# First keys and queries of a hard-max attention kernel: loaded in fp32 from the sync queue and rounded on VectorE and ScalarE instead of cast by the GpSimd queue

## The chip, the cores and the metric

The kernel runs on one core of one Trainium2 chip. The metric is the device time of one execution in microseconds (us), and lower is better. Times below are medians of several executions with their lowest and highest value; no execution showed the slower state of the chip, and for one core a single run's state can't be told ("unknown"). A profiled execution gives a span that is 1.7 to 2.2 us shorter than the time of the same execution, so spans are compared with spans and times with times. What is read from one trace (starts of tiles, landings) belongs to that one execution.

Engine names as the profile has them: PE is TensorE (matmuls), PEld its weight loads, DVE is VectorE, ACT is ScalarE, POOL is GpSimd, SP is SyncE. A name with a q (SPq, POOLq) is an engine's sequencer: it issues transfers, waits on semaphores and so on.

## The reference

```python
def reference(q, k, v):            # B=4, Sq=Sk=4096, D=128, all fp32
    logits = np.matmul(q, k.transpose(0, 2, 1))
    best = np.argmax(logits, axis=-1)
    b_idx = np.arange(q.shape[0])[:, None]
    return v[b_idx, best, :].astype(np.float32)
```

For each query the one key with the largest dot product is found, and its row of v is the output.

## The kernel before

Queries are handled in 128 tiles of 128 rows, 32 for each batch. A tile is screened in fp16: PE multiplies it with the keys, ScalarE evicts (A and E below), VectorE folds the result (W) and takes the eight largest entries (MAX8, written to TOP). GpSimd then gathers the candidates' rows for a more exact comparison, and at the end the rows of v that won. Keys of batch 0 are transposed on PE against an identity matrix. Query tiles 0 to 3 too; all later query tiles are transposed by DMA (`turn_q`), from the sync queue.

The parts that matter here, cut:

```python
    def load_k(b, h, x, y):                       # fp32 in DRAM, fp16 in SBUF: cast by GpSimd's queue
        kb = k[b].rearrange("(h p n) d -> p h n d", p=P, n=16)
        nc.gpsimd.dma_start(out=natk[b % 2][:, h, x:y], in_=kb[:, h, x:y])

    def put_k(b, h):                              # differences of keys, stored for the later gathers
        ...
        nc.vector.tensor_tensor(out=kd[:, h], in0=src[:, :, 1:4, :], in1=..., op=OP.subtract)
        nc.sync.dma_start(out=kb16[:, h], in_=kd[:, h].rearrange("p g f d -> p (g f d)"))

    load_k(0, 0, 0, 16)                           # first half of batch 0's keys
    load_q(0, 0, 4)                               # query tiles 0 to 3
    ...                                           # warm-up matmuls on zeros
    masks.make_identity(nc, ident)
    load_k(0, 1, 0, 8)                            # second half, two pieces
    load_k(0, 1, 8, 16)
    load_q(0, 4, 8)
    load_q(0, 8, NQT)
    ...
    for z in (FR, FQ, FK, FV):
        nc.gpsimd.memset(z, 0)
    ...
    def turn_q(b, x, y):                          # query tiles x..y-1, transposed by DMA
        nc.sync.dma_start_transpose(out=qT[b % 2][:, x * P:y * P]..., in_=natq[b % 2][:, x:y, :]...)

    def dpart(t, x):                              # pd matmuls of tile t, ScalarE's eviction to A
        ...
        mm(ps, t, 1 + 2 * x, True)
        nc.scalar.activation(out=A, in_=ps, func=AF.Abs)
    ...
    trn_half(1, 0, ALL, by_act)                   # first half of the keys: PE transposes, evictions
    trn_half(3, 0, ALL, by_dve)
    trn_half(0, 0, ALL, by_act)
    trn_q(0, 4, by_dve)
    trn_half(2, 0, ALL, by_act)
    put_k(0, 0)
    for u in (1, 3, 0, 2):
        trn_half(u, 1, (0, 1))                    # second half, first piece
    trn_half(1, 1, (2, 3), by_act)                # second half, second piece
    ...
    dpart(0, 0)
    dpart(0, 1)
    ...                                           # main loop; in its first 8 steps GpSimd issues
            load_part(1, it, 4)                   #   batch 1's keys, again casting
        if it == 1:
            turn_q(0, 4, 8)
```

## Time and profile before

| | before |
|---|---|
| time, median of 3 runs | 443.31 us (443.29 to 443.79) |
| profiled span | 441.9 us |
| first screening matmul (pd of tile 0) | 12.34 us |
| first MAX8 | 20.72 us |
| first DMA transpose of queries: issued, landed | 11.86, 18.78 us |
| last scatter starts on GpSimd | 437.69 us |
| software DMAs (GpSimd's DMA instructions in the trace) | 309 |

First the DMA view of the kernel before for 14 to 18 us: packets, MB and share of the 16 engines for GpSimd's queue (q0) and the sync queue (q1).

```profile
q0 software_dynamic: 353, 0.39, 71.9%
q1 hardware_dynamic: 680, 0.50, 44.0%
```

Both queues move data in these 4 us.

### The profile page before, as it was taken

Reading aid. Unit: us, or ns where it says so; the run is one execution under the profiler, and the core shown is the slowest. Engines: PE = TensorE matmul, PEld = TensorE weight load, DVE = VectorE, ACT = ScalarE, POOL = GpSimd, SP = SyncE. Lnnn points to the kernel's source line nnn. Section 1 sums busy time; section 2 is a strip of 40 time slices with the busy share of each in tenths; the row PEclk is TensorE's granted clock in tenths of the full one; section 3 lists DMA queues with packets and bytes.
Section 4 is the critical chain, followed back from the end, with each engine's and each line's share of the span. In section 5 each row is a group of like instructions: output and inputs, shape, how many; then the busy total and the mean of one; then the engine's idle time right before and its main releaser. Section 6 shows DMA issues by size and latency. Waiting matters only on the chain.

```text
span 441.9 us, 6163 instructions
## 1 busy us (share of the span) xinstructions
PE 378.9 (86%) x1830; PEld 168.0 (38%) x1830; DVE 405.9 (92%) x734; ACT 375.6 (85%) x437; POOL 306.2 (69%) x335
## 2 busy tenths in 40 slices
PE   7999999999999999999998889999889997892100
PEld 4444444444444444444443334443333333330100
DVE  2688999999999999999999999999999999999840
ACT  2899999999999999999998889999989998892000
POOL 8413456677768786777777776777777777777673
PEclk9999999999999999999999999999999999998555
DMA  7933999463326999743336993453322332323432
GB/s 123 202 101 65 157 148 139 106 130 80 108 58 134 180 163 170 147 114 91 84 94 142 173 162 100 96 132 107 85 82 84 90 89 80 88 80 102 122 113 53
DMA packets 52868, 50.54 MB, mean 114 GB/s; under 512 B 34136, under 2 KB 40890, under 8 KB 52832
## 3 DMA queue, kind: packets, MB, share of 16 engines
q0 software_dynamic: 19072, 33.87, 39.2%
q1 hardware_dynamic: 33760, 16.26, 14.5%
q8 instruction: 14, 0.23, 0.2%
q14 instruction: 22, 0.18, 0.2%
HBM read 40.05 MB, written 14.55 MB: 124 GB/s over the span
## 4 chain that ended last, share of the span: by engine, by line
ACT 37%; issue 20%; DVE 13%; PE 12%; POOL 8%; DMA 8%; POOLq 0%; ACTq 0%; DVEq 0%; SPq 0%
ACT A L234 31%; ACT E L247 6%; DVE TOP L264 4%; PE psn L225 4%; POOL vr L342 4%; PE pd L225 4%; POOL kg L282 4%; DVE W L260 4%; PE psn L244 3%; DMA vr<-in_v_dram,win 3%; DMA natk<-in_k_dram 2%; DMA out_dram<-vr 1%; DMA kg<-k,cand 1%; DVE prod L300 1%; DMA vr<-in_v_dram,win_w 1%
## 5 line engine op out<-in xcount | busy, mean ns | idle before, releaser
L234 ACT ACTIVATE A<-pd 128x1024 f16<-128x1024 f32 x256 | 260.8, 1046 | 12.5 <-PE pd L225 12.0
L282 POOL DMA_INDIRECT kg<-k,cand x126 | 126.4, 1003 | 80.0 <-DVE cand L276 48.7
L260 DVE SCALAR_TENSOR_TENSOR W<-psn,E 128x1024 int16<-128x1024 f32 x128 | 167.1, 1306 | 7.4 <-ACT E L247 5.3
L225 PE MATMUL psn<-kT,qT 128*128 128x512 f16 x512 | 151.9, 378 | 11.4 <-ACT A L234 4.0
L225 PE MATMUL pd<-kT,qT 128*128 128x512 f16 x512 | 151.9, 379 | 8.7 <-ACT A L234 8.2
L264 DVE MAX8 TOP<-W 128x8 f32<-128x1024 f32 x128 | 157.0, 1227 | 0.0
L225 PEld LDWEIGHTS <-qT 128*128 128x128 f16 x1024 | 97.9, 97 | 151.8 <-issue 62.0
L342 POOL DMA_INDIRECT vr<-in_v_dram,win x126 | 125.9, 999 | 40.0 <-issue 36.1
L244 PE MATMUL psn<-A,identh 128*128 128x512 f16 x512 | 152.1, 378 | 0.0
L247 ACT ACTIVATE E<-psn 128x1024 int16<-128x1024 f32 x128 | 132.6, 1036 | 2.3 <-PE psn L244 1.5
L244 PEld LDWEIGHTS <-identh 128*128 128x128 f16 x512 | 49.6, 97 | 60.7
L300 DVE TENSOR_TENSOR prod<-kg,natq 128x768 f16<-128x768 f16 x63 | 34.8, 554 | 0.4 <-DMA kg<-k,cand 0.4
L205 ACT ACTIVATE kT<-uk 128x256 f16<-128x256 f32 x48 | 20.6, 429 | 1.5 <-PE uk L202 1.5
L305 DVE TENSOR_TENSOR p<-prod 128x768 f16<-128x768 f16 (+1 forms) x36 | 18.1, 502 | 0.1
L310 DVE TENSOR_REDUCE D<-p 128x12 f32<-128x384 f16 (+1 forms) x36 | 17.7, 492 | 0.1
L201 PE MATMUL uk<-identh,natk 128*128 128x128 f16 x96 | 15.8, 218 | 0.0
L484 PE MATMUL fp_e<-n_e,tri 128*128 128x1 f32 x2 | 0.6, 364 | 13.5 <-DVE n_e L482 13.5
L202 PEld LDWEIGHTS <-natk 128*128 128x128 f16 x96 | 9.3, 97 | 7.2 <-issue 5.1
L308 DVE TENSOR_TENSOR p<-p 128x384 f16<-128x384 f16 (+1 forms) x36 | 11.9, 330 | 0.1
L66 POOL DMA_DIRECT2D natk<-in_k_dram x19 | 11.3, 599 | 0.8 <-POOLq L890 0.8
L201 PEld LDWEIGHTS <-natk 128*128 128x128 f16 x96 | 9.3, 98 | 5.6
L69 POOL DMA_DIRECT2D natq<-in_q_dram x15 | 9.2, 614 | 0.0
(152 smaller groups left out, 140.1 us busy)
## 6 DMA issues: line engine op xcount, KB each, us to landing
out_dram<-vr SPq DMA_DIRECT2D x31, 256.0 KB, 2.1
natq<-in_q_dram POOLq DMA_DIRECT2D x12, 256.0 KB, 5.3
natk<-in_k_dram POOLq DMA_DIRECT2D x10, 256.0 KB, 4.5
k<-kd SPq DMA_DIRECT2D x18, 128.0 KB, 3.7
k<-natk POOLq DMA_DIRECT2D x6, 384.0 KB, 6.4
kg<-k,cand POOLq DMA_INDIRECT x126, 3.0
vr<-in_v_dram,win POOLq DMA_INDIRECT x126, 2.7
natk<-in_k_dram POOLq DMA_DIRECT2D x8, 128.0 KB, 5.7
```

Source lines behind the costliest of these rows:

```text
L201: nc.tensor.matmul(out=o, lhsT=natk[b % 2][:, h, 4 * m + x, :], rhs=identh, start=True, stop=False)
L205: nc.scalar.activation(out=kT[b % 2][:, c:c + 256], in_=ps, func=AF.Copy)
L225: nc.tensor.matmul(out=ps[:, n * 512:(n + 1) * 512], lhsT=qT[b % 2][:, qt * P:(qt + 1) * P], rhs=kT[b % 2][:, u * 1024 + n * 512:u * 1024 ...
L234: nc.scalar.activation(out=A, in_=ps, func=AF.Abs)
L244: nc.tensor.matmul(out=ps[:, n * 512:(n + 1) * 512], lhsT=identh, rhs=A[:, n * 512:(n + 1) * 512], start=False, stop=True)
L247: nc.scalar.activation(out=E, in_=ps, func=AF.Relu, scale=QSCALE)
L260: nc.vector.scalar_tensor_tensor(out=W_t[t % NW].bitcast(I16)[:, 1::2], in0=ps, scalar=QSCALE, in1=E, op0=OP.mult, op1=OP.max)
L264: nc.vector.max(out=TOP[:, t, :], in_=W_t[t % NW].bitcast(FP32))
L282: near_q.append(lambda j=j: nc.gpsimd.indirect_dma_start(out=kg[:, j].rearrange("p f d -> p (f d)"), out_offset=None, in_=k16[t0 // NQT], ...
L300: nc.vector.tensor_tensor(out=prod[:, i:i + h], in0=kg[:, i:i + h], in1=natq[b % 2][:, x + i - b * NQT:x + i + h - b * NQT, :].unsqueeze(2 ...
L305: nc.vector.tensor_tensor(out=p1, in0=prod[:, :, :, 0:64], in1=prod[:, :, :, 64:128], op=OP.add)
L342: late_q.append(lambda j=j: nc.gpsimd.indirect_dma_start(out=vr[:, j, :], out_offset=None, in_=v_flat, in_offset=IOA(ap=win[:, i + j:i + j ...
```

## The change

The first keys and queries shall not wait for the casting loads. They are loaded unconverted by the sync queue and rounded to fp16 on chip. GpSimd's zero fills go to ScalarE, which is idle then. The other query loads are issued behind the constants, and the subtraction with its store (`put_k(0, 0)`) moves behind the first screening matmuls.

```diff
-    load_k(0, 0, 0, 16)
-    load_q(0, 0, 4)
+    wide_k = bp.tile([P, 2, 16, P], FP32, tag="wide_k")
+    wide_q = bp.tile([P, 4, P], FP32, tag="wide_q")
+    first_k = k[0].rearrange("(h p n) d -> p h n d", p=P, n=16)
+    nc.sync.dma_start(out=wide_k[:, 0, 0:8], in_=first_k[:, 0, 0:8])
+    nc.sync.dma_start(out=wide_k[:, 0, 8:16], in_=first_k[:, 0, 8:16])
+    nc.sync.dma_start(out=wide_q, in_=q[0].rearrange("(p t) d -> p t d", p=P)[:, 0:4])
+    nc.sync.dma_start(out=wide_k[:, 1, 0:8], in_=first_k[:, 1, 0:8])
+    nc.sync.dma_start(out=wide_k[:, 1, 8:16], in_=first_k[:, 1, 8:16])
...
     masks.make_identity(nc, ident)
-    load_k(0, 1, 0, 8)
-    load_k(0, 1, 8, 16)
-    load_q(0, 4, 8)
-    load_q(0, 8, NQT)
...
-    for z in (FR, FQ, FK, FV):
-        nc.gpsimd.memset(z, 0)
+    nc.gpsimd.memset(FR, 0)
+    for z in (FK[:, 0], FK[:, 1], FK[:, 2], FQ, FV):
+        nc.scalar.activation(out=z, in_=wz[:, 0:z.shape[1]], func=AF.Copy)
+    load_q(0, 4, 8)
+    load_q(0, 8, NQT)
...
+    def narrow(put, h, x, y):
+        put(natk[0][:, h, x:y], wide_k[:, h, x:y])
+
+    narrow(by_dve, 0, 0, 8)
+    narrow(by_dve, 0, 8, 16)
+    by_act(natq[0][:, 0:4], wide_q)
     trn_half(1, 0, ALL, by_act)
     trn_half(3, 0, ALL, by_dve)
     trn_half(0, 0, ALL, by_act)
+    narrow(by_dve, 1, 0, 8)
     trn_q(0, 4, by_dve)
     trn_half(2, 0, ALL, by_act)
-    put_k(0, 0)
+    narrow(by_dve, 1, 8, 13)
+    narrow(by_act, 1, 13, 16)
...
     dpart(0, 0)
     dpart(0, 1)
+    put_k(0, 0)
```

## The prediction

> **What bounds the kernel now.** I read the page first (busy shares), then the windows view cut at the stages, then the chain that ended last, then the timeline of the first 16 us, where the change acts, and the DMA view of the same stretch.
>
> The columns of the windows view are: stretch, length, then busy us (and count) of PE, PEld, DVE, ACT and POOL, then clock, DMA share and GB/s.
>
> ```profile
> 12.34:27.40 15.06, 14.87 (x67) 6.35 (x67) 11.03 (x13) 14.44 (x16) 3.96 (x8) 1.00 1.02 196
> 27.40:60.00 32.60, 31.10 (x163) 14.34 (x161) 29.34 (x35) 32.60 (x42) 15.49 (x18) 1.00 0.59 101
> 60.00:110.00 50.00, 48.89 (x244) 22.13 (x243) 49.83 (x70) 50.00 (x62) 33.25 (x35) 1.00 0.66 117
> 170.00:250.00 80.00, 76.78 (x378) 34.47 (x377) 79.93 (x126) 77.46 (x94) 59.66 (x62) 1.00 0.57 122
> ```
>
> From 12.34 us the kernel runs at throughput: PE is busy 14.87 of 15.06 us, then ACT 32.60 of 32.60, then VectorE 79.93 of 80.00 deep in the run. The change touches none of the work in those stages; it touches what lies before 12.34. So the question is when the first screening matmul (pd, L225) starts. The chain of waits answers (start, us, what):
>
> ```profile
> 3.67 7.54 DMA natk<-in_k_dram
> 11.21 0.05 issue
> 11.26 0.23 PE tk L183
> ...
> 12.34 0.61 PE pd L225 x2
> 12.94 0.02 issue
> 12.96 1.03 ACT A L234
> ```
>
> The last half-load of batch 0's keys lands at 11.21 us; 1.08 us later, after 16 transposing matmuls and one eviction, pd starts. The timeline shows what else stands in the way:
>
> ```profile
> 1.19 5.24 PE L113 MATMUL warm<-wz 128*128 128x512 f16 x14 [1.19 <-DVE wz L109]
> 6.65 0.23 PE L183 MATMUL tk<-identh,natk 128*128 128x128 f16 x1 [0.22 <-DMA natk<-in_k_dram]
> 9.04 0.95 DVE L75 TENSOR_TENSOR kd<-natk 128x1536 f16<-128x1536 f16 x1
> 9.94 0.23 PE L183 MATMUL tk<-identh,natk 128*128 128x128 f16 x1 [0.83 <-DMA natk<-in_k_dram]
> 11.26 0.23 PE L183 MATMUL tk<-identh,natk 128*128 128x128 f16 x1 [0.25 <-DMA natk<-in_k_dram]
> 11.86 1.36 SPq L208 DMA_TRANSPOSE qT<-natq  x1
> 11.91 1.89 DVE L193 CAST kT<-tk 128x512 f16<-128x512 f32 x3 [1.93 <-PE tk L184]
> ```
>
> The warm-up matmuls hold PE until 1.19 + 5.24 = 6.43, so the first half of the keys could be used at most 0.22 us earlier than it is. The second half costs two waits, for loads at 9.94 and 11.26. So the start is DMA-bound, on the second half only.
>
> **What the Trainium skill says.** (1) DMA: Bandwidth & Descriptors, section "SWDGE vs HWDGE vs iDMA": a cast inside a transfer is for the GpSimd queue only, plain copies go to the sync queue. The trace agrees in form: all natk and natq loads are on POOLq and write fp16. That is why the change needs a rounding step. (2) Same page, "iDMA fabric": a plain load stream from SP with 4 KiB rows alone reached 408.7 GB/s. No plain load stream is in this trace, but the casting loads moved 201 to 205 GB/s of fp16 between 4 and 6 us (windows of one us), which is 402 to 410 GB/s of fp32 read. (3) Same page, "Queues, rings and completion order": each DMA engine takes turns between the queue rows it has work for, so sync loads share engines with whatever GpSimd issues. (4) VectorE: DVE Perf Modes, "Mode 2×_2P": a one-source op from SBUF to SBUF yields two elements per cycle even for fp32 (clock 0.96 GHz). The trace agrees: the 128x128 fp32-to-fp16 copy of the identity starts 0.14 us before the next instruction. At two per cycle its data take 128/1.92 = 0.067 us, leaving 0.07 us of overhead, the same as MAX8 leaves (1.14 us in the chain against 1024/0.96 = 1.07).
>
> **The change, part by part.**
>
> *Loads.* Removed from GpSimd: four casting issues before the iotas (natk 0.73, natq 0.59, natk 1.10 for two; some 2.4 us), with two more natq issues (1.08 us) moved behind the constants. Added: five plain loads on sync. They can be issued right after the start barrier, at about 0.75 us (ACT starts at 0.73, VectorE at 0.86), at some 0.35 to 0.42 us of queue time each (the q32 load later in the run takes 0.425). That one's neighbour, a 256 KB output store, takes a median 2.1 us to landing; at 400 GB/s its bytes are 0.65 us, so about 1.4 us is fixed. The loads are 524, 524, 262, 524 and 524 KB in fp32, 2.36 MB. At 400 GB/s, from 0.75 + 1.4 = 2.15, they land at 3.5, 4.8, 5.4, 6.7 and 8.0 us. The last lands 3.2 us before today's 11.21.
>
> *Rounding.* Keys on VectorE: 128x1024 costs 1024/1.92 + 0.07 = 0.61 us, 128x640 costs 0.40. On ACT: q 128x512 is like today's 128x512 eviction, 0.60; the last 128x384 is about 0.48. The first two key copies (done by 5.5) and the q copy (done by 6.0) lie in front of 6.43, where PE is still warming: free. The other three are on the path.
>
> *Simulated start.* PE begins transposing at 6.43 instead of 6.65, so today's events of the first half all move by -0.22. VectorE: eviction of u=3 ends about 8.2, key copy 8.2 to 8.8, q eviction (0.65) to 9.45, 640-wide copy to 9.87. ACT: third eviction ends 9.74 - 0.22 = 9.52, then the 384-wide copy to 10.0. PE does the first eight tiles from 8.85 to 10.0, partly waiting for PSUM buffers. So the last sixteen matmuls can start at about 10.05 instead of 11.26: **1.2 us earlier**. With the same 1.08 us behind them pd starts at 11.13. The gate is now VectorE and ACT, not the transfer, which has about 1.5 us of slack there.
>
> *Zero fills.* GpSimd loses 0.19 + 1.37 + 0.19 = 1.75 us of memsets; ACT gets three of 512 and two of 128 columns, some 3 x 0.5 + 2 x 0.2 = 1.9 us between the table load's end (2.01) and 4.0, before q arrives: free. GpSimd was not on the path either, except through its issues.
>
> *put_k moved.* The 0.95 us subtraction leaves 9.04, makes room for the key copies, and runs after the three last evictions, from about 12.5 to 13.5. VectorE waits for the first E until 16.77 today (2.75 us idle): free on VectorE. But the order of instructions shows its store ahead of the query transposes on the sync queue.
>
> **Sum:** 443.3 - 1.2 + 0 to 0.3 for what follows (below) = **442.1 us**.
>
> **Rivals.**
>
> *A. The query transposes become the wait.* They were issued at 11.86; now they sit behind the store that waits for put_k, so 13.5 + 0.35 = 13.85. Today's first one lands late:
>
> ```profile
> qT<-natq SPq DMA_TRANSPOSE x1, 6.9
> ```
>
> 13.85 + 6.9 = 20.75. Query tile 4 is first used three rounds after pd; today that is 21.75 (rounds of 2.75 us), or 9.4 after pd, hence 20.5 in the new kernel. A stall of 0.2 us, if landing stays slow. Against it: GpSimd's batch-1 and query loads now start at about 7.5 instead of 13.0 for the former, so the burst that slows the transposes should end near 17.6 (3.8 MB at 400 GB/s after 8.0) instead of 20.8; over the run the median is 5.3 us. I give it 0 to 0.3 us; at worst 1 us, leaving 443.1.
>
> *B. Plain fp32 loads are slower.* The same page of bytes is read, but twice as much is written. If the rate were 270 GB/s, the last load would land at 2.15 + 8.7 = 10.9, the gate would be 11.3 to 11.5, and the gain gone: 443.3 to 443.6. For it: between 6 and 9 us today's loads fall to 103 to 157 GB/s of fp16 with the engines fully busy, for a reason I do not see. Against: the 4 to 6 us figure, and the skill's. One in eight.
>
> *C. VectorE copies run at one element per cycle.* Then 1024 columns cost 1.14 us and 640 cost 0.74; the gate moves to 10.8, the gain shrinks to 0.4: 442.9. The identity copy speaks against it.
>
> *D. The shift does not reach the end.* GpSimd gathers or a late wait could absorb it. But every later start follows from a cross-engine wait or a queue position, none from absolute time, and VectorE is full from 60 to 400 us, so a start d earlier should end d earlier. I allow 0.3 us either way for different interleaving.
>
> **Range and chances.** 1.2 us is 0.27% of the time. Main case 441.8 to 442.4; with A or C up to 443; better if the gate falls to the loads' own time (down to 441.3). Range 441.3 to 443.1. Two per cent would be 8.9 us, more than anything before 12.34 could give short of removing most of it, and no rival costs a third of that: within 2% at 0.98.
>
> **What would show it right or wrong.** In the new profile: the sync loads land by about 8 us (B wrong); key copies of 128x1024 show about 0.6 to 0.7 us (C wrong); the last transposing group starts near 10.05 and waits for ACT or VectorE rather than a DMA; the first pd is at 11.1; no PE wait on qT near 20.5 (A wrong; if seen, its length is A's cost); and every stage after that has the same lengths. It is wrong if pd starts at 11.1 and the end has not moved, or if pd is not earlier than 12.

## More of the kernel before

"Software DMAs" are the transfers that GpSimd issues; in the kernel before, all loads that convert fp32 to fp16 under way are of this kind.

GpSimd issued the casting loads of batch 1's keys only from 13.02 on (timeline):

```profile
13.02 3.28 POOL L66 DMA_DIRECT2D natk<-in_k_dram  x6
```

Then the end: the timeline's last work of GpSimd, and the source view of the kernel's closing line (operation, count, duration in ns as minimum/median/maximum, first and last start).

```profile
437.69 1.02 POOL L541 DMA_INDIRECT out_dram<-FV,rowk_e  x1 [3.77 <-DMA out_dram<-vr]
L901 POOLq DRAIN  x3: 46/109/3253, 437.5 to 441.6; - x3
```

The longest of GpSimd's three DRAIN instructions takes 3.253 us. Its record starts at 437.46, just ahead of the last scatter's, and it is what the closing barrier waits for, apart from 0.37 us behind its end, in which SyncE is later: GpSimd goes on at 441.08.

## The result

| | before | after | difference |
|---|---|---|---|
| time, median of 4 runs of the same rounds | 443.3 (442.78 to 443.79) | 449.94 (449.31 to 450.36) | +6.6 us |
| profiled span | 441.9 | 448.5 | +6.6 |
| first pd matmul | 12.34 | 11.57 | −0.77 |
| MAX8 of tile 0 | 20.72 | 19.96 | −0.76 |
| MAX8 of tile 4 | 32.33 | 36.07 | +3.74 |
| MAX8 of tile 64 | 209.43 | 213.13 | +3.70 |
| MAX8 of tile 124 | 398.36 | 401.83 | +3.47 |
| last scatter starts | 437.69 | 440.49 | +2.80 |
| longest DRAIN of GpSimd | 3.253 | 7.342 | +4.09 |
| software DMAs | 309 | 305 | −4 |

The ratio of the times is 1.0149, with a 95% interval of 1.0131 to 1.0167: within the 2% that count as the same, but outside the predicted range by a wide margin, and slower instead of faster. Ratios here and below are the mean time of one kernel's fast runs over that of the other's of the same rounds, so they are not quite the ratio of the medians quoted.

The start did become earlier, as intended. The windows view of the changed kernel, cut at the same times as the prediction's (same columns), shows in which stage that was lost:

```profile
12.34:27.40 15.06, 11.27 (x45) 4.39 (x43) 8.75 (x11) 11.08 (x12) 0.37 (x1) 0.90 1.11 200
60.00:110.00 50.00, 48.92 (x245) 22.15 (x243) 49.83 (x71) 50.00 (x62) 33.42 (x36) 1.00 0.67 122
170.00:250.00 80.00, 76.74 (x375) 34.49 (x375) 79.97 (x123) 78.16 (x95) 59.98 (x62) 1.00 0.56 121
```

PE was busy 14.87 us of the first stretch before; now it is 11.27, with 45 matmuls instead of 67, at a mean clock of 0.90. In the later stages PE and VectorE are busy as long as before, within 0.05 us. The chain of waits names the loss:

```profile
2.14 6.52 DMA wide_k<-in_k_dram
8.68 0.74 DVE natk L198
...
11.15 1.89 DVE kT L198 x3
13.04 0.86 DVE kd L75
...
14.14 0.12 SPq L78
14.30 10.40 DMA qT<-natq
24.70 0.05 issue
24.75 1.03 PE pd L230 x2
```

The first query transpose is issued at 14.30, takes 10.40 us and lands at 24.70, and tile 4's pd matmul starts on it. The timeline shows the queue order: the store of the key differences, then the transposes.

```profile
13.93 0.33 SPq L78 DMA_DIRECT2D k<-kd  x1
14.30 5.79 SPq L213 DMA_TRANSPOSE qT<-natq  x2
```

The wait itself stands in the waits view (us in total, times, longest):

```profile
PE pd L230 <- DMA qT<-natq: 3.6, 1, 3.6
```

Tile 3's rounds would have let tile 4's pd start near 11.57 + 9.41 = 20.98 (9.41 is the distance in the kernel before, 21.75 − 12.34), so 24.75 is 3.77 us late. With the 0.76 us gained that makes +3.01 for tile 4, and its MAX8 shows +3.74. The remaining 0.73 us fits what follows the stall: for about 3 us (24.4 to 27.6) matmuls take 0.63 us in place of 0.38, at a granted clock of 0.50. From there the delay stays nearly constant for 360 us.

Why the transposes took 10.4 us is visible in the DMA view of the changed kernel, 14 to 18 us:

```profile
q0 software_dynamic: 375, 0.53, 91.6%
...
k<-kd SPq DMA_DIRECT2D x1, 384.0 KB, 7.5
qT<-natq SPq DMA_TRANSPOSE x1, 10.4
```

There is no line of q1 at all: in these 4 us not one packet of the sync queue moved, though a store and a transpose were queued on it from 13.93 and 14.30. GpSimd's queue had the engines for 91.6% of the time. It had been given its next loads early (timeline), because GpSimd was relieved of issues and zero fills:

```profile
9.52 3.19 POOL L66 DMA_DIRECT2D natk<-in_k_dram  x6
```

These are batch 1's keys, not needed for a long time, 3.5 us earlier than before. They took a median 11.9 us to land, against 5.8 before (of those whose landing is on record). The store's first packet starts at 18.3 us, and the transposes' small packets pass only from 20 us on.

At the other end of the program, the timeline's last scatter and the closing line of the changed kernel read:

```profile
440.49 1.02 POOL L546 DMA_INDIRECT out_dram<-FV,rowk_e  x1 [3.38 <-DMA out_dram<-vr]
L916 POOLq DRAIN  x3: 51/109/7342, 440.3 to 448.2; - x3
```

Again three DRAINs, but the longest takes 7.342 us. The two losses add up: the last scatter is 2.80 us later, the drain 4.09 us longer, and of the 0.37 us that GpSimd used to go on waiting for SyncE 0.05 are left: 2.80 + 4.09 − 0.32 = 6.57, the lateness of the barrier (447.65 against 441.08) and of the span. The scatter itself is not slower: by its semaphore it has landed at 442.69, and the drain goes on for 4.9 us more, in which the trace shows no packet of GpSimd's queue (the last one starts at 442.35); before, the scatter landed at 439.96 and the drain ended 0.75 us later. The tail also won something back, +3.47 at tile 124 against +2.80 at the last scatter; why was not looked into.

### The profile page after: what moved, and what is told of

Same layout as the page of the kernel before. It is cut to its first block, busy times and chain, and to the rows that moved or that the text cites. A ratio compares the mean times of both kernels' runs of the same rounds, so it can differ in the third digit from the quotient of the medians.

```text
span 448.5 us, 6172 instructions
## 1 busy us (share of the span) xinstructions
PE 378.8 (84%) x1830; PEld 168.2 (38%) x1830; DVE 409.2 (91%) x738; ACT 378.1 (84%) x444; POOL 302.3 (67%) x328
## 3 DMA queue, kind: packets, MB, share of 16 engines
q0 software_dynamic: 18496, 32.69, 36.5%
q1 hardware_dynamic: 34480, 18.62, 15.9%
## 4 chain that ended last, share of the span: by engine, by line
ACT 40%; issue 19%; DVE 15%; PE 15%; DMA 7%; POOL 1%; POOLq 0%; ACTq 0%; SPq 0%; DVEq 0%
ACT A L239 33%; ACT E L252 7%; PE pd L230 5%; DVE TOP L269 5%; PE psn L230 5%; DVE W L265 4%; PE psn L249 4%; DMA qT<-natq 2%; DMA wide_k<-in_k_dram 1%; DVE prod L305 1%; DMA kg<-k,cand 1%; DMA vr<-in_v_dram,win 1%; DMA FK<-in_k_dram,gb_e 1%; DMA vr<-in_v_dram,win_w 1%; DVE p L310 1%
## 5 line engine op out<-in xcount | busy, mean ns | idle before, releaser
L66 POOL DMA_DIRECT2D natk<-in_k_dram x16 | 9.4, 602 | 0.0
```

## The experiments

Twelve kernels were run, all with correct outputs and without slow runs; three of them (307, 317 and 321 software DMAs) were looked at once only, so that their state is unknown. Two questions were open. For the stall, one theory was the order on the sync queue (Q: the transposes come behind the store), the other the backlog of casting loads on GpSimd's queue (B, in its sharper form B2: whatever GpSimd has queued takes the engines while the transposes want them). For the long drain, theory F was that it depends on the number of GpSimd's instructions or on their fetching, theory N that it depends on the number of software DMAs, which the change lowers from 309 to 305. The expectations name two rivals more: T (another reason, such as a slower landing of the last scatter; as far as the scatter goes the trace above has answered that) and K (something else in the change, such as the sync loads or the zero fills on ScalarE).

### Transposes ahead of the store

```diff
     dpart(0, 1)
+    turn_q(0, 4, 8)
     put_k(0, 0)
...
-        if it == 1:
-            turn_q(0, 4, 8)
```

> The changed kernel, but the first query transpose (tiles 4 to 7) is issued on the sync queue ahead of the store of the first key differences instead of behind it. Theory Q (the sync queue's order is the cause of the 3.6 us wait of PE for query tile 4): issue moves from 14.30 to about 12.1 us, the landing from 24.70 to 19 to 20, before the 21.0 at which tile 4 is wanted; the wait is gone, 445 to 446 us. Theory B (the backlog of casting loads already queued by GpSimd is the cause, whatever the order on the sync queue): the transpose still waits for that backlog, lands at 22 us or later, a wait of 1 us or more stays; 446 to 448 us. Neither theory touches the 3.8 us lost after the last scatter.

Measured: 446.15 us (445.8 to 446.55), ratio 1.0071 (1.0054 to 1.0088). The transpose was issued at 11.61, and the last record of its landing is at 21.50, 9.9 us later: still slow, between what Q and B had named, and just in time. The weight load of tile 4 waited 0.8 us for it and its pd matmul started at 21.54, but MAX8 of tile 4 stood at −0.70 against the kernel before, and so it stayed to tile 88. The order, which moves the issue 2.7 us ahead, is thus worth the stall (+3.74 against −0.70 at tile 4). The drain still took 7.34 us, which explains what is left in the profiled executions: the last scatter −1.68, the drain +4.09, SyncE's wait −0.32, in sum +2.09, the difference of the spans (443.97 − 441.88). The medians differ by 2.99; the profiled execution of this kernel is its fastest, that of the kernel before a slow one.

### Batch 1's key loads held until the store's data are ready

```diff
     nc.vector.tensor_copy(out=rec2[:, :, 1], in_=iota_p.to_broadcast([P, SLOTS]))
+    hold = cp.tile([P, 1], BF16, tag="hold")
+    nc.gpsimd.tensor_copy(out=hold, in_=rec2[:, 0, 1:2])     # VectorE writes rec2 at about 14.0
```

> The changed kernel, but GpSimd waits (a one-column copy that reads what VectorE writes at about 14.0 us) before it issues the six loads of the next batch's keys, so that these queue behind the store and the transpose as in the kernel before, not ahead of them. Theory B (backlog): the store's packets start near 15 us instead of 18.2, the first transpose lands by about 20 us, no wait of PE; 445 to 446 us. Theory Q (order on the sync queue alone): landing stays at 24 to 25 us, 449 to 450 us. The instruction count of GpSimd changes by one or two, so the loss at the end may or may not stay.

Measured: 449.31 us (447.42 to 451.7), ratio 1.014 (1.0123 to 1.0157). The store landed earlier, at 18.78, but the transpose, issued at 14.37, landed at 25.01, as late as ever. So a backlog that stands ahead at the moment of issue is not the whole matter: here the loads came just after the transpose's issue and it was slow all the same. In that form B fell. What remained was that the loads compete during the transposes, which the run with the loads held until the transpose has landed tests (below). In the profiled execution, the slowest of the five, tile 4 was +5.27 late although PE's wait was about the same, 3.8 us: after it the granted clock was 0.50 from 24 to 30 us, twice as long as in the changed kernel.

### Eight more instructions on GpSimd, and 120 more

To the changed kernel eight one-column memsets on GpSimd were added, to the kernel before 120:

```diff
+            if it == 5:
+                pad = cp.tile([P, 8], FP32, tag="pad")            # 120 for the kernel before
+                for z in range(8):
+                    nc.gpsimd.memset(pad[:, z:z + 1], 0.0)
```

> The changed kernel with eight one-column memsets added on GpSimd in a stretch in which it idles, which brings its instruction count from 481 back to the 489 of the kernel before. Theory F (the 3.8 us at the end are an instruction fetch that falls between GpSimd's last drain and the final barrier, because its program became eight instructions shorter): the last drain shrinks from 7.3 to about 3.3 us, 446 us. Theory T (the end is late for another reason, such as slower completion of the last scatter): the drain stays at 7.3 us, 450 us. The wait for query tile 4 stays in both.

> The kernel before with 120 one-column memsets added on GpSimd in a stretch in which it idles. The fetched blocks have 8192 bytes; [...]489 + 120 = 481 + 128. Theory F: the last instructions fall where they fall in the changed kernel, the last drain grows from 3.3 to about 7.3 us and the time to about 447 us, with nothing else changed before the end. Theory T: no change, 443.3 us.

Measured: changed kernel with eight, 449.48 us, ratio 1.0147, drain 7.34 us; kernel before with 120, 442.71 us, ratio 0.999 (0.9974 to 1.0007), drain 3.253 us. The drain did not move in either. As to the number of instructions F is refuted; as to their fetching, the 120 were to bring the last instructions to the same place in a fetched block as in the changed kernel, which rests on a size of an instruction that no run shows. The first run also left +2.16 at tile 4 instead of +3.74. Its stall was much the same (a wait of 3.2 us against 3.6; tile 4's pd started at 24.50 against 24.75), but the granted clock stayed at 1.00 behind it.

### Four software DMAs more, four fewer

Four tiny casting loads (128 rows of 4 elements, never used) were added to the version with the transposes ahead, which brings it from 305 software DMAs back to 309. And in the kernel before, without any part of the change, batch 1's eight key loads were merged into four of twice the size: 305.

```diff
+                pad = cp.tile([P, 4, 4], FP16, tag="pad")
+                for z in range(4):
+                    nc.gpsimd.dma_start(out=pad[:, z], in_=q[0].rearrange(...)[:, 0, 4 * z:4 * z + 4])
```

```diff
-        if it < 8:
-            load_part(1, it, 4)
+        if it < 8 and it % 2 == 0:
+            load_part(1, it, 8)
```

> The changed kernel with the first query transpose ahead of the store on the sync queue (as in e1) and with four tiny casting loads (128x4) added on GpSimd where it idles, which brings its software DMAs from 305 back to the 309 of the kernel before. Theory N (the length of GpSimd's last drain follows from the number of software DMAs issued before it, through the descriptor rings or the eight semaphores that take turns): the last drain falls from 7.34 to 3.25 us and the time to about 442.1 to 442.4 us, 0.8 us under the kernel before. Theory K (the long drain follows from something else in the change, such as the sync loads or the zero fills on ScalarE): drain 7.34, 446.2 us.

> The kernel before with the next batch's key loads issued as four of eight tiles instead of eight of four, so 305 software DMAs instead of 309 and the same bytes. Theory N: the last drain grows from 3.25 to 7.34 us and the time by about 4 us to 447 us, with nothing of the change in it. Theory K: drain 3.25, 443 us.

Measured: with four more, 442.94 us (442.08 to 444.63), ratio 0.9986 (0.9973 to 0.9999). With four fewer, 446.68 us (446.51 to 447.54), ratio 1.0083 (1.0068 to 1.0097). The closing lines, first of the one with four more, then of the kernel before with four fewer:

```profile
L919 POOLq DRAIN  x3: 51/109/3258, 438.5 to 442.6; - x3
```

```profile
L901 POOLq DRAIN  x3: 46/109/7335, 436.5 to 444.4; - x3
```

Four useless transfers make the kernel 3.2 us faster (446.15 to 442.94, in two sets of rounds whose kernel before had 443.16 and 443.32), and four saved ones make the old kernel 3.4 us slower, with none of the change in it. K is refuted, and N is confirmed as far as these runs can tell: the long drain goes with the number of software DMAs and not with fp32 loads, rounding or zero fills. It does not go with their bytes either (the queue moved 33.87 MB both in the kernel before and with the loads merged). But a rival stands untested: the packets of GpSimd's queue, on each run's page, change with the count in every kernel, 144 for each software DMA (18496 at 305, 18784 at 307, 19072 at 309), so that number of DMAs and number of packets can't be told apart. In the profiled run with four more, sync loads straggled (the last landed at 11.03 us), the granted clock was 0.50 from 12 to 14 us, the first pd came at 13.61 and every tile ran 1.75 us behind the kernel before; the fp32 loads do not always come in time.

### Batch 1's key loads held until the first transpose has landed

The store stays ahead of the transpose; GpSimd waits until a column of qT's tile 4 can be read before it issues batch 1's loads.

```diff
     put_k(0, 0)
+    turn_q(0, 4, 8)
...
+    hold = cp.tile([P, 1], FP16, tag="hold")
+    nc.gpsimd.tensor_copy(out=hold, in_=qT[0][:, 4 * P:4 * P + 1])
...
-        if it == 1:
-            turn_q(0, 4, 8)
```

> The changed kernel with the store still ahead of the first query transpose on the sync queue, but GpSimd issues the next batch's key loads only after that transpose has landed (a one-column copy that reads its result). Theory B2 (the transpose is slow because its small packets share the engines with GpSimd's casting loads): without them it lands 3 to 4 us after its issue at 14.3, about 18 us, no wait of PE for tile 4, and the rest runs 0.7 us ahead of the kernel before; time about 446.2 us if the long drain stays. Theory Q (only the place behind the store matters): it still lands after 21 us and PE waits.

Measured: 445.97 us (445.77 to 446.09), ratio 1.0059 (1.0045 to 1.0074). Timeline of SyncE, then the wait of GpSimd, which ends with the transpose:

```profile
13.89 0.33 SPq L78 DMA_DIRECT2D k<-kd  x1
14.26 3.75 SPq L213 DMA_TRANSPOSE qT<-natq  x2
```

```profile
POOL hold L699 <- DMA qT<-natq: 9.0, 1, 9.0
```

The order is that of the changed kernel and the issue time too (14.26 against 14.30), yet the transpose landed at 18.44, after 4.2 us in place of 10.4. PE never waits for it, and the tiles stay 0.8 us ahead up to tile 88. The same trace holds a second comparison, among its transposes of eight tiles each. The one issued at 16.78, before the loads were released at 18.62, landed after 3.1 us; those issued at 18.68 and 20.05, beside the loads, landed after 9.3 and 11.2 us (tile view of qT, 0 to 30 us, all four transposes):

```profile
DMA to landing us min/median/max: 3.1/6.7/11.2
```

So the casting loads on GpSimd's queue make the transposes slow (B2), and the order only decides whether this shows (Q). The drain was again 7.34 us and eats the gain.

### The count varied upwards

> The kernel before with the four tiny casting loads added, 313 software DMAs. If theory N works through the eight semaphores that take turns, 313 stands where 305 stands (both leave 1 when divided by 8) and the drain is 7.34 us, 447 us. If it works through the place in the descriptor rings, nothing says which of 3.25 and 7.34 us comes out. Theory K: 3.25 us, 443 us.

The kernel before with four tiny loads more, 313 in all: 443.41 us (443.23 to 443.52), ratio 1.0001 (0.9987 to 1.0016), drain 3.34 us, neither 7.34 nor quite 3.25. So the drain doesn't repeat every eight transfers: 305 and 313 differ by eight, and theirs are 7.34 and 3.34 us.

> The kernel before with eight tiny loads, 317 software DMAs. Period of 8 is refuted by 313; 317 shows whether the short drain holds on above 313 (3.25 us, 443.3 us) or the long one returns (7.34 us, 447 us).

> The kernel before with twelve tiny loads, 321 software DMAs, 16 more than 305. If the drain follows a cycle of 16 DMAs it is 7.34 us and the time 447 us; if not, 3.25 us and 443.3 us.

With eight more (317) and twelve more (321): 444.25 and 443.74 us, drains of 3.58 and 3.79 us. 321 is 16 above 305, so it doesn't repeat every 16 either.

### Both remedies together

The held loads and the four tiny loads, 309 in all; and the same with only two tiny loads, 307:

> The candidate: e7 (GpSimd holds the next batch's key loads until the first query transpose has landed) with four tiny casting loads added so that 309 software DMAs are issued. If both causes found so far are all there is, PE does not wait for tile 4, the rounds run 0.7 to 0.8 us ahead of the kernel before, the last drain is 3.25 us and the time 442.0 to 442.5 us, about 1 us under the kernel before. If the stall or the drain comes back, or a straggling sync load as in the profiled run of e5 is common, it ties at 443 us or more.

> The same with two tiny loads, 307 software DMAs. If the long drain starts below a number between 305 and 309, 3.25 or 7.34 us here halves the range. If it belongs to single numbers such as 305 (1 more than a multiple of 16), 3.25 us. Otherwise as the candidate.

Measured with four: 442.39 us (441.91 to 443.25), ratio 0.9976 (0.9962 to 0.9989), drain 3.26 us. This beats the kernel before by some 0.8 us, about what the change gains at its start (0.5 to 0.8 us, see below). In its profiled run (443.09 us) a new loss appears between tiles 4 and 8, where it goes from −0.66 to +0.42. The timeline of PE names it:

```profile
31.51 0.23 PE L206 MATMUL uk<-identh,natk 128*128 128x128 f16 x1 [1.03 <-DMA natk<-in_k_dram]
```

The held loads are batch 1's keys, which PE transposes piecewise from here on; in this run the transposes landed near 20.0 us, the loads were issued from 20.21 on, and PE had to wait 1.03 us for one. Holding back a transfer has its own deadline.

With two tiny loads, in one run: 448.28 us, drain 7.51 us; its tiles were late as well, +1.69 at tile 24. Here too PE waited 0.9 us for batch 1's keys, and the last sync load had landed late, at 10.55 us.

All counts together:

| software DMAs | drain, us | seen in |
|---|---|---|
| 305 | 7.33 to 7.34 | six kernels, one of them the kernel before with merged loads |
| 307 | 7.51 | one |
| 309 | 3.25 to 3.26 | kernel before, with 120 memsets, the two with four tiny loads |
| 313 | 3.34 | one |
| 317 | 3.58 | one |
| 321 | 3.79 | one |

The drain grows slowly with the count and falls by some 4.2 us between 307 and 309 (307, 317 and 321 rest on one execution each). What it counts, software DMAs or their packets, is open.

## Why the prediction was wrong

The prediction said 442.1 us, between 441.3 and 443.1. The time was 449.94.

**The gain at the start: right in kind, too large.** The 1.2 us were 0.77. The term that was mis-sized is the loads' landing. The last was to land at 8.0 and landed at 9.89 us; the second key piece, the queries and the third key piece (5.97, 6.61 and 8.66 for 4.8, 5.4 and 6.7) also came 1.2 to 2 us late. Reckoned as the prediction did, from 2.15 us, the 2.36 MB came at 305 GB/s, not 400: between the main case and Rival B's 270, and nearer to the latter. The steps "the gate is now VectorE and ACT, not the transfer" and "free", for the copies of the first half, failed with it. PE's warm-up ended at 5.72 instead of 6.43, but PE then waited 1.4 us in two pieces for keys that VectorE rounded as they landed. By the chain shown above, the third key piece (landed 8.66, rounded until 9.41) sets the time from there on. The last piece was ready only just in time: ScalarE's copy waits for the load, and VectorE's can't start before it either (timeline):

```profile
9.91 0.52 ACT L195 ACTIVATE natk<-wide_k 128x384 f16<-128x384 f32 x1 [0.57 <-DMA wide_k<-in_k_dram]
```

```profile
9.93 0.48 DVE L198 CAST natk<-wide_k 128x640 f16<-128x640 f32 x1
```

The last sixteen transposing matmuls could start at about 10.45 and started at 10.50 instead of 10.05, and pd came at 11.57 instead of 11.13.

The 0.77 comes from one pair of traces. In the six traced kernels whose start is that of the kernel before, the first pd starts between 11.98 and 12.34, median 12.20; in the eight with the changed start between 11.54 and 13.61, median 11.67. So the usual gain is nearer to 0.5 us.

**The rounding: right.** Key copies of 128x1024 were predicted at 0.61 us of pitch; where an instruction follows directly, the trace has 0.65, and those of the experiments 0.61 to 0.70 (0.69 to 0.80 as busy time in the trace). Rival C, one element per cycle, is refuted.

**Zero fills: free**, as predicted; no wait at the start names them. But the sentence "GpSimd was not on the path either, except through its issues" had the point in its last words and went no further. Fewer tasks on GpSimd let it issue batch 1's loads at 9.52 instead of 13.02, into the time of the transposes.

**Rival A: the right mechanism, the wrong size.** The issue time was near (predicted 13.85, measured 14.30). But the landing time of 6.9 us was taken over from the kernel before, with the argument that the burst would start earlier and so end near 17.6. The step that failed is that one: the burst did not end near 17.6, five of batch 1's six loads landed between 21.5 and 24.5, and the transpose took 10.4 us. (The old burst's end was put too early as well: in the kernel before GpSimd's queue moved packets until 22.1, not 20.8.) "0 to 0.3 us; at worst 1" was 3.77 us, and some 0.7 more for the lower clock after the stall. With the same order and the loads held, it took 4.2 us. That the earlier loads compete with the transposes, and don't just clear the way sooner, was argued the wrong way round.

**Rival D: right for the stages, wrong for the end.** A delay of 3.7 us at tile 4 was still 3.5 at tile 124; every stage has its old length. "A start d earlier should end d earlier" fails after the last tile, because the prediction has no term at all for the closing drain. This is the missing step: taking four transfers off GpSimd's queue costs 4.09 us there. The change could not have won even without the stall: 0.8 us gained against 4.09 lost. Nothing of the kernel before's profile would have told this number; only the two source-view lines side by side did.

**What stays open.** Why the drain falls between 307 and 309 software DMAs, whether it is their number or that of their packets, and whether it rises and falls again at other counts. Why the granted clock fell to 0.50 behind the stall in two traces and not in a third (+3.74, +5.27 and +2.16 at tile 4 after waits of 3.6, 3.8 and 3.2 us). Why single fp32 loads straggle (11.03 and 10.55 us in two runs). The held kernel's 1.03 us wait was seen in one profiled run; how often it occurs was not measured.

## What to carry to other kernels

Relieving an engine that issues transfers makes its next transfers start earlier; before doing so, look at what they will meet in the same microseconds, and hold back those that have time. A transfer time taken from the old profile is only good while its neighbours on the DMA engines stay the same. And compare the last microseconds of two traces, behind the last useful instruction: four transfers fewer moved the end by 4 us here.

## What the Trainium skill lacked or had wrong

- DMA: Bandwidth & Descriptors, section "SWDGE vs HWDGE vs iDMA", gives plain loads to the sync queue and says that GpSimd's descriptors go through rings in SBUF (the rings that two of the expectations name). Nothing there tells that the length of GpSimd's last DRAIN goes with the number of software DMAs: 7.33 to 7.51 us at 305 and 307, 3.25 to 3.79 us at 309 to 321. Whether the rings have to do with it no run here shows.
- The same page, "Queues, rings and completion order", has each DMA engine take turns between the queues that it has work for. Here a store and a transpose issued on the sync queue at 13.93 and 14.30 had no packet between 14 and 18 us, while GpSimd's queue was busy for 91.6% of the engines' time. Turns, if they were taken, were not taken within 4 us; whether the descriptors had reached the engines by then is not in the trace.
- The same page, "DMA Transpose (X-bar)", gives constraints and alternatives but no time (elsewhere the page has a rate for a transpose, not a landing time), and nothing on how long it takes beside other transfers: the transpose of four query tiles landed after 4.2 us with batch 1's casting loads held back and after 10.4 us beside them.
- The same page, "iDMA fabric", has 408.7 GB/s for a load stream from the sync engine with 4 KiB rows and 1 MiB transfers. In the first 10 us of the changed kernel four loads of 512 KB with such rows and one of 256 KB, no long stream, alone on the two queues until 9.6 us, moved 221 to 426 GB/s in the single microseconds from 2 to 9 us, 322 on average. So the page's figure is too high for a start of this kind.
